# RWKV-7 scan of a two-layer backbone on one core: state kept in PSUM, G products by row halves, triangular blocks of six items inverted together

## The chip, the cores and the metric

The kernel runs on one core of a Trainium2 chip. The metric is device time in microseconds for one launch, which computes the whole two-layer backbone. The kernel before took 4388.3 us, the median of three runs (4386.0 to 4389.41).

The engines are called by the profile's names: PE multiplies matrices, and PEld is its loading of weights; DVE, ACT and POOL work element by element; SP issues the DMA transfers. An instruction on an engine starts after the one before it on that engine, and when the semaphores it waits for are set.

## What is computed

A latent stream of 1024 tokens and a context of 256 tokens, both 1024 wide, go through two layers. Layer 0 is attention beside an mLSTM, and an MLP. Layer 1 is an RWKV-7 mixer in both directions, and an MLP. The change lies in the scan of layer 1. The reference runs it token by token, for 16 heads of width 64:

```python
def rwkv7_scan(r, w, k, v, a, b, state, reverse, with_out):
    ...
    def step(s, inp):
        rt, wt, kt, vt, at, bt = inp
        sa = jnp.einsum('bhij,bhj->bhi', s, at)
        s = s * wt[:, :, None, :] + sa[..., None] * bt[:, :, None, :] + vt[..., None] * kt[:, :, None, :]
        y = jnp.einsum('bhij,bhj->bhi', s, rt) if with_out else None
        return s, y
    state, ys = lax.scan(step, state, tuple(time_major(t) for t in (r, w, k, v, a, b)), reverse=reverse)
    return (jnp.moveaxis(ys, 0, 1) if with_out else None), state
...
    k_dir = k[None] * (1.0 + (a - 1.0) * k_a)
```

Each direction first runs over the context, whose outputs aren't needed, and then over the latent tokens from the state it has reached.

## The kernel before

**Tiling.** The kernel works in chunks of 64 tokens: 4 of the context and 16 latent ones. A *unit* is one pair of heads (128 channels, the two heads in partitions 0 to 63 and 64 to 127) in one direction: 16 units of 20 chunks. An *item* is four chunks of one unit: 80 items, five for each unit. Two units, the two directions of one pair of heads, run together (GROUP), and their items alternate in the list. Within a chunk the recurrence becomes matrix products and the inverse of a 64x64 unit triangular matrix for each head; from chunk to chunk goes the state Z, 128x128 with one 64x64 block per head.

All operands are fp32. A product of the program is two PE instructions with a weight load each, a transpose is one.

**Four kinds of work**, each a Python generator, which yields between its steps:

- `item_a` (L1408) prepares an item. ACT makes the decay factors E and EI; DVE and POOL make kd, q, and the operands BK (128 channels x 4 chunks x 128: b and k side by side) and AR (a and r). ACT copies each head's half of BK into a tile of its own that is zero in the other half (BZ, L1452). PE multiplies BZ with AR over all 128 channels (L1461): eight products, four chunks for each of two heads, with a yield after every second. DVE masks a head's bank of products into the SBUF tile G (L1464). SP writes the two 32x32 diagonal blocks of each triangle to DRAM (ga, L1468). PE transposes BK (L1471), and ACT copies that to BKt (L1474). With the last item of a batch, SP reads the diagonal blocks of all the batch's items into P, one block per partition (L1479).
- `batch_b` (L1482) inverts these blocks, 16 per item, all of a batch at once: 31 steps of two DVE instructions (L1498, L1499), one partition per block. A batch has five items, so 80 partitions. P and R have one buffer each. SP writes R to DRAM (rt, L1502).
- `item_c` (L1507 on) reads an item's inverses back into TT and joins the 32x32 blocks to 64x64 ones: a DVE transpose (L1520), eight 32x32 products Q (L1525), an ACT copy, eight products T (L1530), an ACT copy.
- `unit_chain` (L1536) is the serial part: 20 steps for each unit. A step adds AR times Z to px (L1568), which ACT copies to xs (L1570); PE multiplies xs with TT (L1580), ACT copies that to UV (L1581); PE adds UV times BKt to pz (L1590), and ACT copies pz to the next Z. After odd steps this copy has a scale for each channel, the decay of two chunks (L1593); after even ones it has none (L1595). At the start of an even step pz takes a new bank, and the current Z is put into it by a product with the identity (L1573). The part of px that doesn't need Z is made a step ahead (L1555). For latent chunks py gives the output (L1601, L1603, copied by ACT at L1606).

A pair of heads that is done goes through `readout`, and its result to DRAM.

**What sets the order.** `rwkv_scan` (L1685) gives each generator a start and a step width in units of its own; a heap takes the next one by that time. An item has T = 12 units: the chain takes item e at 12 e, with 2 units from yield to yield and three yields in a step; `item_a` starts at 12 e - 134 (12 e - 126 in the first batch) with steps of 1.8; the inversion of the batch that begins with item a starts at 12 a - 66 with steps of 0.9. This is the order of priority. At compile time the framework then lays out each engine's instructions, and one that is ready may be put ahead of one that waits; on the chip that order is fixed. PSUM has eight banks, all in one pool, and a bank is free again when what was last read from it has been read. G, AR and BKt have PB = 14 buffers, so `item_a` runs up to 14 items ahead of what the chain has finished.

## Time and profile before

| | us |
|---|---|
| median of three runs | 4388.3 |
| the profiled execution | 4391.1 |
| its span, first to last instruction | 4389.3 |
| PE busy | 4121.9 (94%) |
| DVE busy | 2576.4 (59%) |
| ACT busy | 1690.6 (39%) |
| POOL busy | 1300.2 (30%) |
| first G product starts, in the scan | 2605.5 |
| last inversion ends | 3480.9 |

A group's row in the profile names the line, the engine, the operation, what is written and read, the shapes, the count, then the busy time in us and the mean of one in ns, and after the next bar the engine's idle time ahead of these instructions and what ended it. A timeline's row has the start, the duration (from the first start to the last end, if several instructions were merged), engine, line and count. A matmul's end is modelled and lies some 0.2 us after the next one may start, so the time that matmuls hold PE is read from start to start. A row of the windows has a stretch, its length, and the busy time of PE, PEld, DVE, ACT and POOL with the counts, then the granted clock of PE, the DMA engines' busy share and GB/s.

### The profile page before, as it was taken

Reading aid. Unit: us, or ns where it says so; the run is one execution under the profiler, and the core shown is the slowest. Engines: PE = TensorE matmul, PEld = TensorE weight load, DVE = VectorE, ACT = ScalarE, POOL = GpSimd, SP = SyncE. Lnnn points to the kernel's source line nnn. Section 1 sums busy time; section 2 is a strip of 40 time slices with the busy share of each in tenths; the row PEclk is TensorE's granted clock in tenths of the full one; section 3 lists DMA queues with packets and bytes.
Section 4 is the critical chain, followed back from the end, with each engine's and each line's share of the span. In section 5 each row is a group of like instructions: output and inputs, shape, how many; then the busy total and the mean of one; then the engine's idle time right before and its main releaser. Section 6 shows DMA issues by size and latency. Waiting matters only on the chain. (4 is left out here: it accounts for less than half of the span.)

```text
span 4389.3 us, 71617 instructions
## 1 busy us (share of the span) xinstructions
PE 4121.9 (94%) x27565; PEld 3323.6 (76%) x27565; DVE 2576.4 (59%) x4890; ACT 1690.6 (39%) x4095; POOL 1300.2 (30%) x1530
## 2 busy tenths in 40 slices
PE   6999998998999999997979986999999998999999
PEld 3899876666777888875757765888888865888887
DVE  4320366517555666669684437777777535666666
ACT  4132365522111111126655444666666632111111
POOL 4111010114111111106533444455555323222221
PEclk9999999999999999998979997999999999999999
DMA  4414255401221111111343553444444331111111
GB/s 172 119 60 139 86 160 159 169 29 44 77 87 58 39 39 39 35 65 49 101 123 104 174 179 102 116 123 131 130 129 128 92 125 44 48 48 48 48 49 63
DMA packets 389185, 409.15 MB, mean 93 GB/s; under 512 B 149884, under 2 KB 305820, under 8 KB 388844
## 3 DMA queue, kind: packets, MB, share of 16 engines
q1 hardware_dynamic: 388844, 404.58, 30.6%
q8 instruction: 217, 3.56, 0.3%
q14 instruction: 124, 1.02, 0.1%
HBM read 304.71 MB, written 95.57 MB: 91 GB/s over the span
## 5 line engine op out<-in xcount | busy, mean ns | idle before, releaser
L280 DVE SCALAR_TENSOR_TENSOR x<-m,mods,x 128x512 f32<-128x512 f32 x1280 | 823.7, 690 | 572.4 <-PE m L110 572.0
L95 POOL TENSOR_TENSOR wl<-raw,wh 128x1024 fp32r<-128x1024 f32 (+1 forms) x236 | 507.2, 2152 | 1922.7 <-ACT wh L94 1898.7
L94 ACT ACTIVATE wh<-raw 128x1024 fp32r<-128x1024 f32 (+1 forms) x236 | 221.5, 940 | 1368.7 <-PE m L110 1068.7
L110 PE MATMUL m<-h,wh 128*128 128x512 f32 (+1 forms) x2560 | 633.3, 375 | 26.1 <-POOL h L229 18.4
L110 PEld LDWEIGHTS m<-h,wh 128*128 128x128 f32 x2560 | 450.8, 189 | 148.1 <-POOL h L229 28.5
L110 PE MATMUL m<-hidh,wh 128*128 128x512 f32 x1280 | 357.9, 372 | 5.7 <-DVE x L280 5.7
L110 PE MATMUL m<-hidl,wh 128*128 128x512 f32 x1280 | 355.4, 371 | 0.8 <-DVE hidl L267 0.7
L110 PE MATMUL m<-hidh,wl 128*128 128x512 f32 x1280 | 352.8, 370 | 0.0
L110 PE MATMUL m<-h,wl 128*128 128x512 f32 x1280 | 352.8, 372 | 0.0
L377 PE MATMUL pt<-wh,h 128*128 128x256 f32 x1600 | 289.3, 283 | 0.0
L110 PEld LDWEIGHTS m<-hidh,wh 128*128 128x128 f32 x1280 | 224.5, 188 | 56.5 <-DVE x L280 13.7
L110 PEld LDWEIGHTS m<-hidl,wh 128*128 128x128 f32 x1280 | 224.8, 188 | 44.6 <-DVE hidl L267 2.2
L110 PEld LDWEIGHTS m<-h,wl 128*128 128x128 f32 x1280 | 225.4, 189 | 42.4
L110 PEld LDWEIGHTS m<-hidh,wl 128*128 128x128 f32 x1280 | 224.3, 188 | 42.9 <-issue 0.5
L377 PEld LDWEIGHTS pt<-wh,h 128*128 128x128 f32 x1600 | 250.0, 192 | 0.0
L1461 PE MATMUL G<-AR,BZ 128*128 128x128 f32 x1280 | 230.6, 305 | 19.5 <-POOL EI L1432 6.2
L377 PE MATMUL pt<-wl,h 128*128 128x256 f32 x800 | 226.4, 283 | 0.0
L1498 DVE TENSOR_TENSOR prd<-P,R 80x31 f32<-80x31 f32 (+15 forms) x496 | 207.8, 419 | 22.5 <-DMA P<-ga 10.1
L1499 DVE TENSOR_TENSOR R<-R,prd 80x31 f32<-80x31 f32 (+15 forms) x496 | 204.9, 413 | 6.9
L1461 PEld LDWEIGHTS G<-AR,BZ 128*128 128x128 f32 x1280 | 175.4, 199 | 43.3 <-issue 8.2
L1018 POOL TENSOR_TENSOR ss<-h 128x512 f32<-128x512 f32 (+1 forms) x128 | 152.9, 1203 | 123.0 <-DVE xt L1021 98.8
L1464 DVE TENSOR_TENSOR G<-G,c_gmask 128x512 f32<-128x512 f32 (+1 forms) x160 | 101.1, 634 | 140.0 <-PE G L1461 140.0
(406 smaller groups left out, 8302.9 us busy)
## 6 DMA issues: line engine op xcount, KB each, us to landing
raw<-in_w SPq DMA_DIRECT2D x128, 512.0 KB
araw<-in_ada_w SPq DMA_DIRECT2D x80, 512.0 KB
kar<-rw_kar SPq DMA_DIRECT2D x64, 384.0 KB
css<-rw_css SPq DMA_DIRECT2D x80, 256.0 KB
x<-in_xT SPq DMA_DIRECT2D x16, 640.0 KB
raw<-in_w_v SPq DMA_DIRECT2D x20, 512.0 KB
rw_css<-rs SPq DMA_DIRECT2D x16, 640.0 KB
UV<-rw_v SPq DMA_DIRECT2D x80, 128.0 KB
```

Source lines behind the costliest of these rows:

```text
L94: self.nc.scalar.activation(hi, raw, AF.Copy)
L95: (eng or self.nc.gpsimd).tensor_tensor(lo, raw, hi.bitcast(F32), ALU.subtract)
L110: mm(o[:M, :b - a], ww, xx[:, a:b], start=(first and p == 0), stop=(last and p == 2))
L280: V.scalar_tensor_tensor(xt[c][:, u:v], p[:, u - a:v - a], gate[:, c, cond:cond + 1], xt[c][:, u:v], ALU.mult, ALU.add)
L377: mm(ps[:, :n], xx[:, sl], ww[:, k % 4, :], start=(k == 0 and p == 0), stop=(k == KC - 1 and p == 2))
L1018: nc.gpsimd.tensor_tensor(S, h[:, q - 1:q - 1 + w], h[:, q + 1:q + 1 + w], ALU.add)
L1461: nc.tensor.matmul(ps[:, 128 * j:128 * j + 128], BZ[h][:, j, :], AR[:, j, :], start=True, stop=True)
L1464: V.tensor_tensor(G[:, :, h, 0:m], ps.rearrange("q (c t) -> q c t", t=128)[:, :, 0:m], mask[:, :, 0:m], ALU.mult)
L1498: V.tensor_tensor(pr, P3[:, s, s + 1:32].unsqueeze(1).to_broadcast([n_, w, n]), R3[:, 0:w, s].unsqueeze(2).to_broadcast([n_, w, n]), ALU.mult)
L1499: V.tensor_tensor(R3[:, 0:w, s + 1:32], R3[:, 0:w, s + 1:32], pr, ALU.add)
```

## The change

- *G products*: BZ and its copies go. Each head's products contract that head's 64 channels alone, from BK and AR directly, in that half of the PE rows, into two banks, one for each head, both taken at the start. The two heads alternate. A block has four products instead of two. The transposes of BK and their copies to BKt stand directly behind the second block. `item_a` has four yields instead of seven.
- *kd* is made by ACT instead of DVE.
- *State in PSUM*: pz takes a bank and the identity product once for a unit, at n = 0. After odd steps ACT scales pz in place, besides writing the scaled Z.
- *Batches* have NI = 6 items instead of five: thirteen of six and one of two. `item_a` starts 12 units earlier, with steps of 3.0, and G, AR and BKt have 15 buffers instead of 14.

```diff
-PB = 14
+PB = 15
+NI = 6
...
-    V.tensor_scalar(kd, sa, C["k_a"][:, p:p + 1], C["omk"][:, p:p + 1], ALU.mult, ALU.add)
+    nc.scalar.activation(kd, sa, AF.Identity, scale=C["k_a"][:, p:p + 1], bias=C["omk"][:, p:p + 1])
...
-    BZ = kk.BZ[kk.rr % 2]
-    kk.rr += 1
-    for h in range(2):
-        nc.scalar.activation(BZ[h][HH[h]].rearrange("q c t -> q (c t)"), BK[HH[h]].rearrange("q c t -> q (c t)"), AF.Copy)
     yield
...
-    for h in range(2):
-        ps = kk.bank("G")
-        for j in range(4):
-            nc.tensor.matmul(ps[:, 128 * j:128 * j + 128], BZ[h][:, j, :], AR[:, j, :], start=True, stop=True)
-            if j % 2:
-                yield
+    pg = [kk.bank("G") for _ in range(2)]
+    for j in range(4):
+        for h in range(2):
+            nc.tensor.matmul(pg[h][:, 128 * j:128 * j + 128], BK[HH[h], j, :], AR[HH[h], j, :], start=True, stop=True)
+        if j == 1:
+            yield
+    pt = kk.bank("bkt")
+    for j in range(4):
+        nc.tensor.transpose(pt[:, 128 * j:128 * j + 128], BK[:, j, :], kk.ident)
+    for h, ps in enumerate(pg):
         V.tensor_tensor(G[:, :, h, 0:m], ps.rearrange("q (c t) -> q c t", t=128)[:, :, 0:m], mask[:, :, 0:m], ALU.mult)
+    del pg
+    t = it.BKt = kk.tmb([128, 4, 128], "BKt", bufs=PB)
+    for j in range(0, 4, 2):
+        nc.scalar.activation(t[:, j:j + 2].rearrange("q c t -> q (c t)"), pt[:, 128 * j:128 * j + 256], AF.Copy)
     yield
     for d in range(2):
         B = slice(32 * d, 32 * d + 32)
         nc.sync.dma_start(b.ga[d][:, it.e].rearrange("s c t -> s c t"), GA[B, :, :, B].rearrange("s c h t -> s (c h) t"))
-    pt = kk.bank("bkt")
...
     yield
...
-        if n % 2 == 0:
+        if n == 0:
             pz = kk.bank("pz")
             nc.tensor.matmul(pz[:, 0:128], kk.ident, Z, start=True, stop=False, skip_group_check=True)
...
-                nc.scalar.activation(Zn, pz[:, 0:128], AF.Copy, scale=u.items[(n + 1) // 4].wl[:, w:w + 1])
+                f = u.items[(n + 1) // 4].wl[:, w:w + 1]
+                nc.scalar.activation(Zn, pz[:, 0:128], AF.Copy, scale=f)
+                nc.scalar.activation(pz[:, 0:128], pz[:, 0:128], AF.Copy, scale=f)
...
-    kk.BZ = [[kk.tmx([128, 4, 128], "BZ%d%d" % (z, i), bufs=1) for i in range(2)] for z in range(2)]
...
-        n = min(sizes.pop(0) if sizes else 5, len(items) - a)
+        n = min(sizes.pop(0) if sizes else NI, len(items) - a)
...
-        jobs.append((T * (e - it.e) + AS * it.e - (134 if e > it.e else 126), 1, 1.8, it.a))
+        jobs.append((T * (e - it.e) + AS * it.e - ((134 if e > it.e else 126) + AS * (NI - 5)), 1, 3.0, it.a))
```

## Prediction

> **What bounds the kernel now.** I read the page's forty slices first, then the busy times of the scan (the stretch from about 2600 to 3545 us; the change touches nothing outside it), then the groups and the timeline inside it.

> ```profile
> PE   6999998998999999997979986999999998999999
> ```

> ```profile
> core 0: us, PE busy (x) PEld busy (x) DVE busy (x) ACT busy (x) POOL busy (x), PEclk, DMA share, GB/s
> 2700.00:3400.00 700.00, 694.59 (x8393) 587.75 (x8393) 538.16 (x1400) 472.98 (x1491) 374.98 (x759) 1.00 0.47 123
> 3011.00:3055.60 44.60, 44.10 (x548) 37.18 (x548) 41.10 (x109) 30.00 (x95) 26.11 (x48) 1.00 0.48 133
> 3055.60:3063.80 8.20, 8.16 (x84) 6.77 (x84) 2.07 (x6) 5.81 (x20) 5.75 (x13) 1.00 0.56 121
> ```

> From 2700 to 3400 us PE is busy 694.6 of 700 us at a granted clock of 1.00: PE sets the pace. But DVE, 77% over the stretch, is 92% busy while it inverts a batch (41.10 of 44.60) and 25% in the gap before the next batch (2.07 of 8.20). It is the next bound.

> ```profile
> 2731.70 0.79 SPq L1479 DMA_DIRECT2D P<-ga  x1
> ...
> 3386.32 1.92 SPq L1479 DMA_DIRECT2D P<-ga  x2
> ```

> These loads begin batches of five items. The first and last are twelve batches apart: 654.6 / 60 = 10.9 us per item. That period is what the change must shorten.

> What PE spends on an item is read from start to start, since ends are modelled:

> ```profile
> 3005.23 0.49 PE L1461 MATMUL G<-AR,BZ 128*128 128x128 f32 x2
> 3005.65 0.43 PE L1568 MATMUL px<-Z,AR 128*64 128x128 f32 x2
> 3006.01 0.71 PE L1573 MATMUL pz<-Z,ident 128*128 128x128 f32 x4
> 3006.56 0.39 PE L1461 MATMUL G<-AR,BZ 128*128 128x128 f32 x2
> ...
> 3009.56 0.39 PE L1603 MATMUL py<-UV,G 128*64 128x64 f32 x4
> 3009.88 0.71 PE L1461 MATMUL G<-AR,BZ 128*128 128x128 f32 x4
> 3010.52 0.65 PE L1568 MATMUL px<-Z,AR 128*64 128x128 f32 x4
> 3011.32 0.68 PE L1580 MATMUL px<-xs,TT 128*64 128x64 f32 x8
> 3012.35 0.34 PE L1590 MATMUL pz<-UV,BKt 128*64 128x64 f32 x4 [0.36 <-ACT UV L1581]
> ...
> 3059.75 0.40 PE L1555 MATMUL px<-UV,G 128*64 128x64 f32 x4
> 3059.98 0.40 PE L1580 MATMUL px<-xs,TT 128*64 128x64 f32 x4
> ```

> A G block of four instructions holds PE 0.64 us (3009.88 to 3010.52), one of two 0.42 (3005.23 to 3005.65): 0.11 per instruction and **0.20 per block**, whatever its size. The block ahead of it is stretched too: four instructions of 64 columns take 0.32 with G behind them (3009.56 to 3009.88), but 0.23 with their own shape behind them (3059.75 to 3059.98), so 0.09 is the change of shape. A small block between steps of the chain thus pays 0.29 before it has done any work.

> **The change, part by part.**

> ```profile
> L1461 PE MATMUL G<-AR,BZ 128*128 128x128 f32 x1026 | 185.8, 299 | 0.0
> L1573 PE MATMUL pz<-Z,ident 128*128 128x128 f32 x232 | 44.7, 306 | 0.0
> ```

> These groups are of 2700 to 3400 us. Eight products of two instructions make 16 per item: 64 items.

> *G products.* An item's products stand in four blocks now: 4 x 0.64 = 2.56 us. Afterwards each product contracts 64 rows, the two heads' in different halves of the array, and a block has four products. Do two halves run side by side? One line elsewhere does it:

> ```profile
> 503.63 2.21 PE L799 MATMUL s<-aq 64*128 64x256 f32 x16
> ```

> Sixteen instructions of 64 rows and at least 256 columns are 4096 columns in 2.21 us, 0.54 ns a column, tail included; G's 0.11 us for 128 columns is 0.86. In line they would take 3.5 us, so pairs overlap. I take the new block at four pair times, 4 x 0.11 + 0.20 = 0.64 (ends: 0.64, and 8 x 0.11 + 0.20 = 1.08 without overlap). Two such blocks: 1.28 us. Gain 1.28, and two stretched neighbours fewer, 0.18: **1.46 us per item**.

> The bkt transposes go right behind the second block. They are of the full shape, the products of the half shape, so I leave their own 0.20 in place. [...]

> *pz kept in PSUM.* The identity product that put Z back into pz goes, except at n = 0: 232 / 64 = 3.6 instructions per item, 0.9 of a block of 0.55 (3006.01 to 3006.56) and its neighbour's 0.09: **0.58 us per item**. In its place ACT scales pz in place after each odd step.

> ```profile
> L1452 ACT ACTIVATE BZ<-BK 64x512 f32<-64x512 f32 x128 | 79.7, 623 | 1.7
> L1593 ACT ACTIVATE Z<-pz,wl 128x128 f32<-128x128 f32 x116 | 40.3, 366 | 5.7 <-PE pz L1590 4.8
> L1595 ACT ACTIVATE Z<-pz 128x128 f32<-128x128 f32 x128 | 34.0, 277 | 42.6 <-PE pz L1590 41.4
> L1433 ACT ACTIVATE EI<-css 128x256 f32<-128x256 f32 x64 | 26.7, 417 | 1.5
> ```

> No row shows an activation from PSUM to PSUM; the nearest are L1595 (0.28, no scale operand) and L1593 (0.37, the same scale operand). I take 0.37. ACT per item: 473.0 / 64 = 7.39 now; minus two BZ copies 1.25, plus kd at EI's 0.42, plus 116 / 64 x 0.37 = 0.66: 7.2. No relief: on a shorter item it is busier. Behind the scale wait yt and the second unit's Z, so that unit's next px product starts 0.37 later, at most 0.37 us per item (two odd steps in an item, two units that step together). G blocks cover it where one stands there; I take 0.15.

> *Waits that appear.* Two items have four steps of three hand-overs PE to ACT to PE, twelve gaps. Fillers now: 8 G blocks, 2 bkt, 2 Q, 2 T, 2 identity. Afterwards: 4 G (two with bkt), 2 Q, 2 T. Four gaps lose their cover. An uncovered one is visible: L1568's four start at 3010.52, hold 0.44 of work, and L1580 comes at 3011.32: 0.36 lost, as before L1590. Four of these are 0.72 us per item; some gaps are open already, so I take half, 0.36 (ends 0 and 0.72).

> *DVE.* kd goes to ACT, and batches hold six items:

> ```profile
> L1498 DVE TENSOR_TENSOR prd<-P,R 80x247 f32<-80x247 f32 (+15 forms) x400 | 168.6, 421 | 6.0 <-DMA P<-ga 0.5
> L1499 DVE TENSOR_TENSOR R<-R,prd 80x247 f32<-80x247 f32 (+15 forms) x399 | 167.3, 419 | 5.2
> L1429 DVE TENSOR_SCALAR kd<-css,c_k_a,c_omk 128x256 f32<-128x256 f32 x64 | 33.3, 520 | 0.2
> L1464 DVE TENSOR_TENSOR G<-G,c_gmask 128x512 f32<-128x512 f32 (+1 forms) x128 | 81.7, 638 | 125.5 <-PE G L1461 125.5
> ```

> One inversion is 31 x (0.421 + 0.419) = 26.0 us whatever its rows (96 instead of 80; the elements along each row stay). Per item 5.2 becomes 4.3, minus 0.52 for kd: 538.2 / 64 = 8.4 becomes 7.0. Is that enough? Let an item take t. The inversion's stretch is 6t - 8.2, in it 26.0 and 2.7 per item of other work, at 92%: this closes at t = 8.5. With five items it would close at 9.75. So the batch of six gains little by itself; it keeps DVE from taking over.

> *Moved.* The two ga transfers, and the P loads behind them, are issued from the same generator; it starts one item earlier and has fewer steps. SP issues the same number per item and the P loads are fewer, so I cost that at nothing; the cover is the 92% stretch, and what would be late is P.

> *Buffers.* One more of G, AR, BKt goes with the start one item earlier:

> ```profile
> L1442 POOL TENSOR_TENSOR AR<-kar,E 128x256 f32<-128x256 f32 x64 | 54.9, 857 | 97.9 <-PE py L1601 87.8 <-PE px L1568 10.1
> ```

> POOL waits for an AR that the chain frees; with both shifted by one item it waits as before. Cost nothing.

> *Start and end.*

> ```profile
> 2598.69 1.92 POOL L1693 MEMSET BZ<- 128x512 f32 x4
> ...
> 2616.47 0.60 PE L1471 MATMUL bkt<-ident,BK 128*128 128x128 f32 x4
> ...
> 2619.94 0.60 PE L1471 MATMUL bkt<-ident,BK 128*128 128x128 f32 x4
> ```

> The first inversion waits for one item more, 3.5 us; the BZ memsets (1.9) go: +2 (ends -3, if the freed DVE shortens the first inversion, and +4).

> ```profile
> L1573 PE MATMUL pz<-Z,ident 128*128 128x128 f32 x54 | 10.6, 312 | 0.0
> L1461 PE MATMUL G<-AR,BZ 128*128 128x128 f32 x56 | 10.5, 300 | 0.0
> ```

> After 3400 us (these rows) there are 13 identity blocks, 8 us by starts; PE waits there for the chain, so I take 3.

> **The sum.** Per item 1.46 + 0.58 - 0.15 - 0.36 = 1.53 us, a period of 9.4. G instructions after 2700 us: 1026 + 56 = 1082, 67.6 items; one more is done before the chain starts: 66.5. 66.5 x 1.53 = 102; with 3 and -2, 103 us. The profiled execution took 4391.1 (span 4389.3 and 1.8 around it): 4288. The median shown is 4388.3, 2.8 lower: **4285 us**.

> **The rivals.**

> *DVE takes over* (0.20). Per item DVE is busy 8.4, idle 1.96 for G products (125.5 / 64) and 0.57 otherwise. If idle time stays per item, 7.0 + 2.5 = 9.5; and the masks now stand in the same step as the products, both after the second block, so the wait may grow to 9.9. For: 92% in the inversion. Against: the gap's 25%. Saving 1.0 x 66.5: about 4322.

> *All gaps stay covered* (0.08). No wait is added: 2.04 x 66.5 + 6 = 142: 4247.

> *The halves don't overlap* (0.03): the change wouldn't do what it says. Blocks of 1.08, 1.28 falls to 0.40: 0.65 per item, 43 us: 4345. Against it stands L799.

> *PSUM banks run out* (0.05), the slower side. There are eight banks in one pool. pz now holds two for whole units, G takes two at once and keeps both until DVE has masked them; px takes two to four, py two, and bkt and Q or T one each. If the chain's next px must wait for a mask queued behind inversion work on a DVE that is 92% busy, the whole chain waits. It decides from 1.53 us of stall per item; three inversion operations and two masks, 3 x 0.42 + 2 x 0.64 = 2.5 us, would make (2.5 - 1.53) x 66.5 = +65: 4453. Against: pz holds its two nearly always already, and nothing on PE waits for a mask now. [...]

> **How the numbers follow.** Forecast 0.62 (own range 4255 to 4315), DVE 0.20, covered 0.08, halves 0.03, banks 0.05, and 0.02 that gains and waits cancel. From 4235 to 4345 lie all cases but the banks, the cancelled one and the tails. A measurement of this kernel tells about 0.2% from no change; faster 0.93, within it 0.02, slower 0.05.

> **What would show it.** G blocks of eight instructions 0.6 to 0.7 us from start to start, starts in pairs; identity products only at n = 0; P loads of full batches some 56 us apart, six items each; DVE near 75% between them. Wrong: PE idle before L1568 or L1580 released by DVE or by banks; DVE at 90% throughout; G blocks of 1.1 us; a first chain step much later than before.

## The result, and the profile after

| | kernel before | changed kernel |
|---|---|---|
| median | 4386.2 us (5 runs) | 4407.9 us (5 runs, 4403.9 to 4413.1) |
| ratio to before, 95% interval | | 1.0051 [1.0038, 1.0064] |
| span of the profiled execution | 4389.3 us | 4406.1 us |

The change makes the kernel 0.5% slower; 4285 was forecast, from 4235 to 4345. One run of e18, the last experiment below, took 5437.7 us at a granted clock of 0.68 and is left out of its median. The windows of the changed kernel, over the stretch that the prediction read:

```profile
2700.00:3400.00 700.00, 639.09 (x8011) 538.98 (x8008) 470.25 (x1181) 433.39 (x1516) 338.89 (x735) 0.91 0.46 120
```

PE, 694.6 us busy at a clock of 1.00 before, is now idle for 60.9 us, and its granted clock is 0.91 on average. The second number is the surprise: no term of the prediction has the clock in it. The page's row of the clock in forty slices, the kernel before's first, shows where: the scan lies in the slices from the twenty-fourth to the thirty-third, and in four of these (24, 27, 30 and 33) the digit has fallen.

```profile
PEclk9999999999999999998979997999999999999999
...
PEclk9999999999999999999979977989989989999999
```

The loads of P show the pace. The first of these belongs to a full batch, the other to the full batch ten later:

```profile
2740.84 1.24 SPq L1478 DMA_DIRECT2D P<-ga  x2
...
3418.27 1.47 SPq L1478 DMA_DIRECT2D P<-ga  x2
```

677.4 us for 60 items are 11.3 us an item, instead of 10.9; 9.4 was forecast. (Counted by G products, as below, it is 11.1 over 700 us.) The groups of 2700 to 3400 that answer to the prediction's rows, and last the kernel before's row of Q:

```profile
L1497 DVE TENSOR_TENSOR prd<-P,R 96x252 f32<-96x252 f32 (+15 forms) x324 | 144.1, 445 | 6.0 <-DMA P<-ga 0.2
L1498 DVE TENSOR_TENSOR R<-R,prd 96x255 f32<-96x255 f32 (+15 forms) x325 | 138.7, 427 | 5.9
...
L1458 PE MATMUL G<-AR,BK 64*128 64x128 f32 x1008 | 135.5, 330 | 0.0
...
L1572 PE MATMUL pz<-zero,ident 128*128 128x128 f32 x24 | 6.2, 341 | 0.0
...
L1594 ACT ACTIVATE pz<-pz,wl 128x128 f32<-128x128 f32 x114 | 38.1, 334 | 0.0
...
L1465 DVE TENSOR_TENSOR G<-G,c_gmask 128x512 f32<-128x512 f32 (+1 forms) x126 | 77.6, 632 | 174.1 <-PE G L1458 174.0
...
L1524 PE MATMUL Q<-T,G 32*32 32x32 f32 x1008 | 45.5, 197 | 40.2 <-DVE T L1519 34.5 <-DVE rds L1660 4.0 <-DVE prd L1497 1.7
...
L1525 PE MATMUL Q<-T,G 32*32 32x32 f32 x1024 | 43.9, 192 | 0.5 <-DVE prd L1498 0.5
```

G's 1008 instructions are 63 items. The identity products are gone but for n = 0, and ACT's scaling costs 0.33 us. New are the waits ahead of Q: PE is idle there for 40 us, in the kernel before for 0.5. DVE is what it waits for, and DVE, by the row of the masks, stands idle for 174 us ahead of them, waiting for PE's G products (125.5 before).

One of these stalls, in the timeline of the changed kernel; DVE, SP and PE together, by time:

```profile
3152.04 0.35 DVE L1497 TENSOR_TENSOR prd<-P,R 96x192 f32<-96x192 f32 x1
...
3152.32 0.92 SPq L1516 DMA_DIRECT2D TT<-rt  x2
...
3155.30 0.71 PE L1458 MATMUL G<-AR,BK 64*128 64x128 f32 x6
...
3155.84 0.69 DVE L1465 TENSOR_TENSOR G<-G,c_gmask 128x512 f32<-128x512 f32 x1 [3.45 <-PE G L1458]
...
3158.30 0.57 PE L1589 MATMUL pz<-UV,BKt 128*64 128x64 f32 x8
...
3162.23 0.42 DVE L1519 STREAM_TRANSPOSE T<-TT 32x256 f32<-32x256 f32 x1
...
3162.80 1.03 PE L1524 MATMUL Q<-T,G 32*32 32x32 f32 x16 [3.94 <-DVE T L1519]
```

TT's load was issued at 3152.3, so what the transposition needed was soon there. But DVE's order has a mask first, and DVE stood 3.45 us until PE came to that G block; then it worked without a pause through masks, inversion and readout and reached the transposition at 3162.2. PE had been standing since 3158.9. Two engines, each in a fixed order, waited for each other in turn.

At some batches' first items the inversion itself is late (rows by time):

```profile
2792.30 0.33 SPq L1501 DMA_DIRECT2D rt<-R  x1
...
2792.77 0.57 PE L1589 MATMUL pz<-UV,BKt 128*64 128x64 f32 x8
...
2795.39 0.80 SPq L1516 DMA_DIRECT2D TT<-rt  x2
...
2798.04 1.03 PE L1524 MATMUL Q<-T,G 32*32 32x32 f32 x16 [4.70 <-DVE T L1519]
```

PE finishes what it has 1 us after the inverses are written, and Q can start only 5.7 us after that writing. Five first items stand before Q in these 700 us. At two of them the inverses were 5.7 and 8.1 us old; at the other three they were nearly 16 us old or older, so there it wasn't the inversion's end that Q waited for. What follows shows in the windows around it (busy time of PE, PEld, DVE, ACT and POOL, then the clock):

```profile
2792.80:2795.30 2.50, 0.54 (x8) 0.37 (x8) 1.34 (x4) 1.27 (x5) 1.81 (x6) 1.00 0.70 183
2795.30:2798.70 3.40, 0.66 (x13) 0.69 (x14) 0.43 (x1) 0.00 (x0) 1.10 (x2) 0.50 0.73 130
2798.70:2802.10 3.40, 3.40 (x37) 2.82 (x35) 0.00 (x0) 1.02 (x3) 0.00 (x0) 0.50 1.29 182
2802.10:2805.50 3.40, 3.40 (x34) 3.18 (x34) 0.00 (x0) 0.81 (x3) 0.00 (x0) 0.50 0.14 45
```

From 2795.3 us, where PE stands, its granted clock is 0.50, and it is 0.50 still for the 6.8 us of full work behind the stall. A G block of eight then takes far longer:

```profile
2789.77 0.71 PE L1458 MATMUL G<-AR,BK 64*128 64x128 f32 x8
2790.42 0.66 PE L1463 MATMUL bkt<-ident,BK 128*128 128x128 f32 x4
...
2802.08 1.23 PE L1458 MATMUL G<-AR,BK 64*128 64x128 f32 x8
2803.24 0.69 PE L1579 MATMUL px<-xs,TT 128*64 128x64 f32 x4
```

0.65 us from start to start at a clock of 1.00 (as forecast), 1.16 at 0.50.

**Where the time went.** For 2700 to 3400 us I split an item's time in three: PE idle (700 less PE's busy time), loss by the clock (0.40 of the time in which PE was busy at half clock), and what is left, PE's work at full clock. The 0.40 is an estimate, set by the run with the kernel before in batches of six (e8 below), whose work must be the kernel before's: 0.40 gives 10.85 for 10.81, and 0.42 would give 10.81. All in us for an item:

| kernel | period | PE idle | clock loss | PE's work |
|---|---|---|---|---|
| before | 10.92 | 0.08 | 0.02 | 10.81 |
| changed | 11.11 | 0.97 | 0.71 | 9.44 |
| e1: changed, five items | 11.29 | 0.99 | 0.88 | 9.42 |
| e2: changed, 14 buffers | 12.61 | 2.52 | 0.56 | 9.53 |
| e3: five items, 14 buffers | 10.61 | 0.58 | 0.46 | 9.56 |
| e16: before, pz kept in PSUM | 11.63 | 0.63 | 0.61 | 10.39 |
| e8: before, six items | 13.43 | 1.92 | 0.66 | 10.85 |
| e14: changed, Q waits for nothing late | 11.07 | 0.68 | 0.77 | 9.62 |
| e17: changed, idle product added | 11.68 | 0.64 | 0.91 | 10.13 |
| e18: e3, idle product added | 11.27 | 0.37 | 0.36 | 10.53 |

PE's work fell by 1.37 us an item; 0.89 came back as idle time and 0.69 as clock. In e1 to e3, and in e14, PE's work is within 0.2 us of the changed kernel's: what tells these versions apart is how long PE stands and how long it runs at half clock.

### The profile page after: what moved, and what is told of

Same layout as the page of the kernel before. It is cut to its first block, busy times and chain, and to the rows that moved or that the text cites. A ratio compares the mean times of both kernels' runs of the same rounds, so it can differ in the third digit from the quotient of the medians.

```text
span 4406.1 us, 70815 instructions
## 1 busy us (share of the span) xinstructions
PE 4077.6 (93%) x27277; PEld 3278.8 (74%) x27277; DVE 2514.6 (57%) x4686; ACT 1653.6 (38%) x4159; POOL 1274.5 (29%) x1522
## 5 line engine op out<-in xcount | busy, mean ns | idle before, releaser
L110 PEld LDWEIGHTS m<-hidh,wh 128*128 128x128 f32 x1280 | 224.1, 188 | 54.2 <-DVE x L280 11.5
L1497 DVE TENSOR_TENSOR prd<-P,R 96x31 f32<-96x31 f32 (+19 forms) x434 | 186.9, 431 | 19.7 <-POOL R L1493 11.2
L1458 PE MATMUL G<-AR,BK 64*128 64x128 f32 x1280 | 170.7, 344 | 20.6 <-POOL AR L1447 8.6
L1498 DVE TENSOR_TENSOR R<-R,prd 96x31 f32<-96x31 f32 (+19 forms) x434 | 183.3, 422 | 8.3
L1458 PEld LDWEIGHTS G<-AR,BK 64*128 64x128 f32 x1280 | 121.4, 220 | 50.6 <-POOL AR L1447 12.2
```

Of the source, the lines that this page charges most:

```text
L110: mm(o[:M, :b - a], ww, xx[:, a:b], start=(first and p == 0), stop=(last and p == 2))
L1458: nc.tensor.matmul(pg[h][:, 128 * j:128 * j + 128], BK[HH[h], j, :], AR[HH[h], j, :], start=True, stop=True)
L1497: V.tensor_tensor(pr, P3[:, s, s + 1:32].unsqueeze(1).to_broadcast([n_, w, n]), R3[:, 0:w, s].unsqueeze(2).to_broadcast([n_, w, n]), ALU.mult)
L1498: V.tensor_tensor(R3[:, 0:w, s + 1:32], R3[:, 0:w, s + 1:32], pr, ALU.add)
```

## The experiments

Line numbers of the runs differ by one or two from those of the changed kernel. All ratios are to the kernel before, run beside it on the same chip, with 95% intervals.

**How many items, how many buffers.** Four runs of the changed kernel with other constants:

```diff
 e1                  e2                  e3                  e4
-PB = 15, NI = 6    -PB = 15, NI = 6    -PB = 15, NI = 6    -PB = 15, NI = 6
+PB = 15, NI = 5    +PB = 14, NI = 6    +PB = 14, NI = 5    +PB = 15, NI = 4
 start 12 e - 146    start 12 e - 134    start 12 e - 134    start 12 e - 146
```

> The changed kernel with batches of five, still 15 buffers and the start 12 units earlier. Theory A (a closed loop sets the pace: the chain frees an item's AR buffer, the last item of a batch takes it, its G, P, the inversion, TT, and the chain goes on; 92.7 us in the changed kernel, and the chain can do PB - NI - 1 = 8 items meanwhile): 9 items fit now, 92.7 / 9 = 10.3 us an item instead of 11.3, some 66 us less, about 4340 us, and the stall of some 10 us once in a batch shrinks. Theory B (DVE's work sets it): five items carry 26 us of inversion instead of six, 0.87 us per item more on DVE, so the same or slower, 4408 to 4465. Theory C (the lost covers between PE and ACT in the chain set it): no change, 4400 to 4415.

> The changed kernel with 14 buffers and the start of item_a put back by 12 units, batches of six kept. Theory A: only 7 items fit into a loop of 92.7 us, 13.2 us an item, some 130 us more, about 4535. Theories B and C: nothing that DVE or the chain's steps do is changed, 4400 to 4415.

> The changed kernel with batches of five and 14 buffers, as before the change: G by halves, pz kept and kd on ACT alone. Theory A: PB - NI is as in the changed kernel, 8 items for the loop; DVE's inversion stretch keeps its 44 us: the same within 1%, 4370 to 4420, so batches of six brought nothing. Theory B: slower by 0.87 us an item, about 4465. Theory C: 4400 to 4415.

> The changed kernel with batches of four, 15 buffers and the early start. Theory A with DVE as the next bound: the loop has 10 items, 9.3 us an item, but four items must carry 26 us of inversion at 92% beside 2.7 us of other work each: DVE closes at 11.5 us an item, so 4400 to 4430, DVE over 85% busy throughout and no stall at the first item of a batch. Theory A without DVE: 4290 to 4330. Theory C: 4400 to 4415 with DVE no busier than now.

Measured: e1 4410.7 us (1.0052 [1.0036, 1.0067]), e2 4505.2 (1.0266 [1.0247, 1.0286]), e3 **4365.6** (0.9945 [0.9929, 0.9962]), e4 4486.2 (1.0217 [1.0200, 1.0235]). e3 beats both kernels: it has the G halves, pz in PSUM and kd on ACT, but the kernel before's batches, buffers and start. The changed kernel is 42 us slower than it. The two constants work only together: with 14 buffers six items cost 140 us more than five (e2 against e3), with 15 and the earlier start they cost nothing (the changed kernel against e1), but there both are slow. e2 comes near what theory A expected (4535), but e1, which has one buffer more than e3 and starts one item earlier, misses its 4340 by 70 us and is 45 us worse than e3. Why more room makes five items slower, no run shows. In e4 P is loaded every 49 us, for four items.

**Six items, and one part, in the kernel before.**

```diff
 e8
-        n = min(sizes.pop(0) if sizes else 5, len(items) - a)
+        n = min(sizes.pop(0) if sizes else 6, len(items) - a)
 e16
-        if n % 2 == 0:
+        if n == 0:
...
+                nc.scalar.activation(pz[:, 0:128], pz[:, 0:128], AF.Copy, scale=f)
```

> The kernel before with batches of six instead of five and nothing else. Theory L: the load of P waits for one item more, so it goes 5.2 items x 10.9 = 57 us ahead of its use instead of 68, where 66 to 72 are needed: a stall of some 10 us a batch and a throttled clock behind it, 13 batches: 4500 to 4560. Rival M: G blocks of four, interleaved with the chain, keep DVE's waits short, so six items alone cost little: 4385 to 4420.

> The kernel before with one part of the change: pz keeps its bank for a unit, the identity product is made at n = 0 alone, and ACT scales pz in place after odd steps. By the terms: 0.58 saved, 0.15 for ACT's scaling, two gaps of twelve uncovered 0.18: 0.25 us for an item, 17 us: 4365 to 4380. Rival: the scaling on ACT costs the chain as much as it saves, or its wait is new on PE before px: 4383 to 4400.

Measured: e8 4568.4 us (1.0422 [1.0406, 1.0439]); e16 4416.0 us (1.0063 [1.0048, 1.0078]), slower where 4365 to 4380 was expected. PE's waits in e8, then in e16 (us in total, times, longest):

```profile
PE Q L1525 <- DVE T L1520: 94.3, 9, 13.0
```

```profile
PE Q L1525 <- DVE prd L1498: 33.0, 11, 3.4
```

In e8 nothing but the batch size differs, and every batch's first Q stands for some 10 us: P waits for one item more. e16 is the clearest run of the study. PE's work fell by 0.42 us an item, 2.1 for a batch of five, and in eleven of the twelve batches whose first Q lies between 2700 and 3400 us PE now stands before it, 3.0 us on average. One of them in e16, DVE, SP and PE by time:

```profile
3180.43 0.33 SPq L1502 DMA_DIRECT2D rt<-R  x1
...
3180.85 3.42 SPq L1479 DMA_DIRECT2D P<-ga  x2
...
3184.26 0.57 PE L1590 MATMUL pz<-UV,BKt 128*64 128x64 f32 x8
...
3184.52 1.36 SPq L1517 DMA_DIRECT2D TT<-rt  x2
...
3186.86 0.19 DVE L1498 TENSOR_TENSOR prd<-P,R 80x31 f32<-80x31 f32 x1 [3.40 <-DMA P<-ga]
...
3187.69 0.42 DVE L1520 STREAM_TRANSPOSE T<-TT 32x256 f32<-32x256 f32 x1
...
3188.26 1.03 PE L1525 MATMUL Q<-T,G 32*32 32x32 f32 x16 [3.44 <-DVE prd L1498]
```

The transposition stands on DVE behind the next inversion's first operations, these wait for the next P, whose one buffer comes free when this inversion ends, and TT's load stands on SP behind P's. From the inverses' writing to Q it takes 7.8 us; PE has work for 4.4. The same place in the kernel before:

```profile
3165.18 0.32 SPq L1502 DMA_DIRECT2D rt<-R  x1
...
3174.24 0.57 PE L1590 MATMUL pz<-UV,BKt 128*64 128x64 f32 x8
...
3174.75 0.67 PE L1525 MATMUL Q<-T,G 32*32 32x32 f32 x16
```

9.6 us from writing to Q, and PE filled all of them with work. So in the kernel before PE was busy all the time, and the way from an inversion to the next Q fitted beside it with 1.8 us to spare here (9.6 less 7.8), and 3.4 at every second batch, where 11.2 us lie between.

This margin alone doesn't give e16's time: 2.1 us less work for a batch against 1.8 and 3.4 would leave a short stall, not a longer period. But e16 lost, for a batch, some 3 us standing and 3 more at half clock. Its inversions, from the fourth to the fourteenth, also took 48 to 55 us from the first operation to the last, instead of 43 to 47, and in them DVE waited 4 to 9 us for G products instead of 1 to 5. That the slowed PE holds up DVE, and DVE holds up PE again, fits these numbers; it is argued, not shown.

**Shorter hand-over, more buffers, less work on DVE.**

```diff
 e5 (the inverses handed over are those after 23 steps)
+        V.tensor_tensor(R3[:, 0:w, s + 1:32] if s < 23 else pr, R3[:, 0:w, s + 1:32], pr, ALU.add)
+        if s == 22: (rt is written here)
 e9 (the last eight steps are left out)
-    for s in range(31):
+    for s in range(23):
 e6
+PB = 16, KB = 2, item_a and batch_b start 12 units earlier, pool WO1 with 3 buffers
```

> The changed kernel, but R is written to DRAM after 23 of the 31 inversion steps; the other eight steps still run on DVE with the same shapes, but add into prd, and no one reads them. So DVE's work is the same, and an inversion's latency is some 8 x 1.4 = 11 us shorter (the inverses are incomplete). Theory L (the loop from the load of P to the use of TT, 66 to 72 us whatever the item rate, no longer fits into the 6.2 items by which P goes ahead): the stalls before Q, 38 us from 2700 to 3400, fall under 6, the granted clock goes from 0.91 to 0.98 or more, and the kernel takes 4295 to 4330. Rival M (DVE in its fixed order stands before the masks until PE has done the products, up to 10 us, and PE before Q for DVE; both move with each other, so a shorter inversion is eaten by longer waits for G): stalls above 25 us, 4385 to 4410.

> The changed kernel with the last eight of the 31 inversion steps left out (the inverses are incomplete). Beside the run with the early hand-over only DVE's work differs: it is 8 x 0.84 = 6.7 us less for a batch, 1.1 us for an item; the hand-over is as early. Theory M (DVE and PE, each in its fixed order, wait for each other in turn: DVE before a mask for the G products, then late with what stands behind, so that the transposition comes late and PE stands before Q): DVE catches up sooner, the stalls of PE from 2700 to 3400 go from 33 us to under 20, the clock to 0.95 or more, 4340 to 4375. Rival L2 (only when TT is loaded counts): nothing changes beside the early hand-over, 4395 to 4410.

> The changed kernel with 16 buffers of G, AR and BKt, items and inversions started 12 units, one item, earlier; for the room kar and css have two buffers instead of three, and the pool for the next phase's weights three instead of four (which may cost some us behind the scan). Theory L: P is loaded 7.2 items ahead of its use instead of 6.2, nearly 10 us more: stalls before Q under 6 us, clock 0.98 or more, 4295 to 4340. Rival M: as in the run with five items and 15 buffers, an earlier start only makes the wait for the products and for TT longer: stalls of 30 us or more, 4390 to 4430.

Measured: e5 4403.6 us (1.0043 [1.0025, 1.0061]), e9 4381.2 (0.9990 [0.9975, 1.0006]), e6 4401.3 (1.0038 [1.0026, 1.0051]). An inversion that hands over some 11 us earlier (the estimate of the expectation) gains 4 us where theory L expected 75 or more, and one more buffer gains 7; the intervals tell neither gain from none. L, that the inversion's latency alone is too long, falls for the changed kernel. PE's waits in e5:

```profile
PE Q L1525 <- DVE T L1520: 22.0, 11, 4.9
```

Of the 12 stalls of 1 us or more before Q in e5, eight are not at a batch's first item: their inverses had been written 30 us and more before. Taking work off DVE helps (e9 against e5, 22 us), as M expects, but less than it expected; e9's profile is of an execution 27 us above its median and doesn't show where.

**Another order.**

```diff
 e7, e12
+    yield
     for h, ps in enumerate(pg):
         V.tensor_tensor(G[:, :, h, 0:m], ...
 e10, e11 (with e3's constants), e12
-        jobs.append((T * e - 11, 3, 2.7, it.c))
+        jobs.append((T * e - 23, 3, 2.7, it.c))
+    (three yields instead of one before the transposition, and three before Q)
```

> The changed kernel with one more yield between the second block of products with its transposes, and the masks, so masks, ga and P come 3 units (2.3 us at 9.4 us an item) later in the order of priority. Theory L: P comes later, the stalls before Q grow by some 2 us a batch: 4410 to 4440. Rival M: DVE's waits for G (174 us from 2700 to 3400) fall by a third or more and the stalls with them: 4330 to 4380.

> The changed kernel; only the order of priority of item_c differs: TT is loaded 23 units ahead of its use instead of 11, the transposition stands 14.9 ahead instead of 8.3, Q 6.8 instead of 5.6. So between transposition and Q lie 8.1 units (6.3 us at 9.4 us an item) instead of 2.7 (2.1 us). Theory M: DVE may be up to 6 us late before PE stands: stalls under 15 us from 2700 to 3400, clock 0.97 or more, 4310 to 4350. Rival L (the inversion's end is too late for the batch's first item, whatever the order): the stalls at first items, about half of all, stay or grow, since DVE now stands before the transposition: 4380 to 4430.

> The same priorities of item_c with batches of five and 14 buffers (the version that takes 4365.6). Theory M: its stalls of 21 us, of which 8 stand before Q, fall by the 8 at most: 4345 to 4360. Rival L: DVE stands before the transposition of first items: 4365 to 4390.

> The run with the transposition apart, and the masks one yield later as well. Theory M: DVE's waits for G fall too, so this is the best of the four: 4300 to 4340. Rival L: P is loaded later, and the first items' stalls grow: 4390 to 4440.

> The version with five items and 14 buffers (4365.6), with the masks one yield later. In the changed kernel this brought 9 us. Theory M: 4345 to 4362, stalls under 21 us. Rival L: P is loaded 2.3 us later; first items wait: 4368 to 4390.

Measured: e7 4399.0 us (1.0034 [1.0022, 1.0047]), e10 4407.0 (1.0037 [1.0023, 1.0052]), e11 4390.8 (1.0011 [0.9998, 1.0023]), e12 4422.7 (1.0071 [1.0053, 1.0089]), e15 (e3 with e7's yield) 4377.7 (0.9976 [0.9965, 0.9987]). None does what M promised. PE's waits in e10:

```profile
PE Q L1526 <- DVE T L1520: 24.4, 4, 8.7
PE px L1556 <- DMA UV<-rw_v: 7.7, 3, 3.1
```

With the transposition far ahead of Q, the stalls in the middle of batches are gone, as M said; all that hold PE over 1 us at Q are at first items, and they are longer, as L said. Both causes are there, and the order that cures the one feeds the other. Moving the masks back by one yield lost 12 us in e3; the 9 us that it gained in the changed kernel lie within the overlap of the two intervals.

**Nothing to wait for.** In e13 every TT is loaded from the first batch's inverses; in e14 Q also multiplies with zeros instead of the transposition's result.

```diff
 e13, e14
-        nc.sync.dma_start(t[B, :, B], b.rt[a:a + 8]...
+        nc.sync.dma_start(t[B, :, B], kk.rt0[a:a + 8]...
 e14
-... T1[S0, e, :], start=True, stop=True, tile_position=(0, 32))
+... kk.zero[S0, 0:32], start=True, stop=True, tile_position=(0, 32))
```

> The changed kernel, but every TT is loaded from the inverses of the first batch, which lie in a DRAM tile of their own, so no item waits for its batch's inversion; all instructions and transfers still run. From 2700 to 3400 us the stalls before Q of the changed kernel are 18 us at a batch's first item and 19 at others. Theory L plus M (first items wait for the inversion, the others for a DVE that is late): the first items' stalls go and the others stay: 15 to 22 us of stalls, clock 0.94 to 0.96, 4340 to 4375. M alone (both kinds come from DVE being late): stalls of 30 us or more, 4390 to 4410.

> The run before, and Q multiplies G with a tile of zeros instead of the transposition's result, so PE waits neither for the inversion nor for the transposition; both still run, and the instructions are the same. If the stalls before Q and the halved clock behind them are what ate the gain: stalls under 5 us, clock 0.99 or more, and the forecast's time: 4280 to 4310. Rival C (PE would then stand elsewhere: before px for masks or UV, or for banks): stalls of 15 us or more at other lines, 4340 to 4390.

Measured: e13 4413.5 us (1.0059 [1.0044, 1.0074]), e14 4381.2 (0.9983 [0.9971, 0.9994]), not the forecast's 4285. e13, in which no item waits for its own batch's inversion, is no faster than the changed kernel; PE still stands 24 us before Q, where L and M together expected 15 to 22 of stalls and M alone 30 or more. PE's waits in e14:

```profile
PE px L1555 <- DMA UV<-rw_v: 8.2, 3, 4.1
PE pz L1590 <- ACT UV L1581: 8.1, 20, 1.1
PE px L1555 <- DVE G L1465: 7.7, 4, 2.3
PE px L1580 <- ACT xs L1570: 6.9, 17, 0.9
```

Rival C it is: Q waits no more, and PE stands before px for a load of UV or a mask, and before the chain's hand-overs. That is less idle time (0.68 us an item instead of 0.97), but the clock's loss isn't smaller. Two windows of e13 show why:

```profile
3002.30:3005.70 3.40, 1.85 (x18) 1.41 (x20) 0.00 (x0) 1.29 (x5) 1.73 (x6) 1.00 1.08 137
3005.70:3009.10 3.40, 3.40 (x30) 2.83 (x28) 0.00 (x0) 0.54 (x2) 0.00 (x0) 0.51 0.79 86
```

No wait in the first is longer than 1 us, yet PE is busy for only 1.85 of 3.40 us, and the next window runs at half clock.

**Useless work.** The identity product is put back, into columns of pz's bank that no one reads (it starts anew in the bank in which pz accumulates; the result is off the reference's, by a relative error of 0.26):

```diff
+        elif n % 2 == 0:
+            nc.tensor.matmul(pz[:, 256:384], kk.ident, Z, start=True, stop=True, skip_group_check=True)
```

> The changed kernel plus useless work: at every even step but n = 0, PE multiplies Z with the identity into 128 columns of pz's bank that no one reads, where and as often as the kernel before put Z into pz: 0.58 us of PE's time for an item, 39 us in all. Theory K (PE loses more by standing than by working: from 2700 to 3400 us each 3.4 us window in which PE was busy less than 60% was followed by one at half clock, and net of stalls and lost clock an item takes 9.5 us now, 10.9 in the kernel before, where neither occurs): at 10.1 us an item the rest keeps up better, stalls halve to 20 us, the clock rises to 0.95 or more, and the useless work costs nothing or brings something: 4365 to 4408. Rival W (stalls come from an order that doesn't fit and stay as they are): the work adds to the time, 4430 to 4450.

> The same useless products in the version with five items and 14 buffers (4365.6; net 9.7 us an item, stalls 21 us, 41 us lost by the clock from 2700 to 3400). Theory K: net 10.3 us, stalls under 8 us, clock 0.98 or more: 4345 to 4370. Rival W: 4390 to 4405.

Measured: e17 4445.3 us (1.0133 [1.0106, 1.0161]), e18 4412.8 (1.0067 [1.0043, 1.0092]). Rival W holds. PE idles less, as K said (0.64 instead of 0.97, 0.37 instead of 0.58), but the product costs more (0.69 and 0.97 us an item) than 0.58, and it waits itself:

```profile
PE pz L1574 <- ACT pz L1596: 5.5, 10, 0.7
```

So giving PE more work doesn't buy back what it loses by standing; with it the new order is only slower.

## Why the prediction was wrong

- *G blocks and overlap of the halves*: right for a block, 0.65 us for eight instructions. But of the two blocks an item 3.3 were made, as PE's order cut them up (210 blocks for the 63 items; 4.5 instead of the four assumed before). From start to start G holds PE 1.92 us an item, from 2.58 before: 0.66 gained, part of it eaten by the half clock, where 1.28 was forecast.
- *pz kept in PSUM*: from 0.62 us an item to 0.09 by starts, 0.53 where 0.58 was forecast; ACT's scaling 0.33 where 0.37 was taken. Both sizes hold, yet e16, which has this part alone, is slower than the kernel before. Together with G and the blocks' neighbours PE's work fell by 1.37 where 2.04 was forecast.
- *Waits that appear*: PE's two main waits for the chain's hand-overs in the changed kernel are

```profile
PE px L1579 <- ACT xs L1569: 10.1, 30, 0.6
PE pz L1589 <- ACT UV L1580: 5.4, 15, 0.6
```

  15.5 us, 0.25 an item; 0.36, and 0.15 for ACT, were forecast. Here the forecast was too dark.
- *Moved* and *Buffers*, both "at nothing": **this is the step that failed.** The prediction said that what would be late is P, and found no cost in it, with the 8.2 us between two inversions taken as given, and the bound of DVE at 9.75 us an item for five, 8.5 for six. So it turned all of PE's saved work, less the chain's hand-overs, into saved time. But the way from an inversion to the next Q, over P, SP's order and DVE's order, had only 2 to 3 us of room: e16, with PE's work 0.42 us an item shorter and nothing else changed but ACT's scaling, stands before the first Q of eleven batches of twelve. In the changed kernel Q's waits cost 40.2 / 63 = 0.64 us an item. Six items cost 182 us in the kernel before (e8); with 15 buffers and the earlier start they cost nothing beside five (e1), but both are 42 us or more behind e3.
- *The clock*: it stood at 1.00 in every sum and had no term, which is the same step's second half, as the windows below show. It cost 0.71 us an item. With Q's waits this is 1.35. The saving of PE's work was put 0.67 too high, and the cost of the hand-overs 0.26 too high, which goes the other way: 1.35 + 0.67 - 0.26 = 1.76, about the 1.73 between the forecast (1.53 less) and the result (0.20 more).
- *Rivals*: "DVE takes over" had the right place (the masks' wait grew from 2.0 to 2.8 us an item), but saw DVE as the bound. It is busy 470 of 700 us, less than before, and one inversion's operations take 31 x (0.445 + 0.427) = 27.0 us where 26.0 was taken. The banks played no part in the stalls that I followed. The slower side, at 0.05, got too little: it was tied to the banks alone.
- *Start and end*: 63 items of 1.73 us too much are 109 of the 120 us by which the profiled execution missed the forecast. The rest lies outside the window. The first chain step came at 2677.8 us, 8 us earlier than before, where 2 later was forecast.

**Open.** Whether any order feeds a PE that needs 9.4 us an item, none of the runs shows: each wait taken away brought up another. That stalls and half clock took the gain is shown by the split of the table, and that half clock follows stalls by the windows below. What makes the stalls is followed in a few places only. Every edit also changes the order that is laid out at compile time, and no run holds that order fixed, so how much of e16's loss, or of e1's, comes from the order alone isn't shown. G by halves and kd on ACT weren't run without pz in PSUM.

## What to carry to other kernels

A busy engine at 100% doesn't mean that it is the only bound: look at how long its next external input has been there when it is used (here the inverses, written 9.6 us before Q and needing 7.8), and don't cost a moved load at nothing while that margin is smaller than what the change saves between two uses. Here PE's clock fell to half behind each of the 13 windows of the changed kernel in which PE was busy for less than 60%, and a G block behind one of them took 1.16 us instead of 0.65; so put a price on each new stall that counts the slow work behind it. And take a change of several parts apart first: e3, with the batches, buffers and start of the kernel before, was the version that paid, and e16 shows that a part that saves work can still cost time.
